# The gate product of a decoder's embedding step: tokens as one 512-column matmul, the sample's tokens as narrow matmuls

## The chip, the cores and the metric

The kernel runs on one core of one Trainium2 chip. The metric is the device time of one execution in microseconds. A core has a matrix engine (TensorE, PE in the profile, with PEld for its weight loads), VectorE (DVE), ScalarE (ACT), GpSimd (POOL) and SyncE (SP), which here issues nearly all DMAs. Each engine has its own instruction stream, run in order; the streams wait for each other by semaphores.

## The reference

One step of a decoder with two layers. The same weights are applied to 512 prompt tokens and to 8 x 4 = 32 sample tokens. The mixing part (a state-space scan and windowed attention) stands between two half-step FFNs; behind them comes a per-layer input embedding, whose gate is what is changed here:

```python
def _layer(h, pe, ssm0, conv0, k_past, v_past, pos0, lp):
    h = h + (0.5 * _swiglu(_rmsnorm(h, lp['g_ffn1']), lp['w1_a'], lp['w3_a'], lp['w2_a'])).astype(hd)
    ...
    h = h + mix.astype(hd)
    h = h + (0.5 * _swiglu(_rmsnorm(h, lp['g_ffn2']), lp['w1_b'], lp['w3_b'], lp['w2_b'])).astype(hd)
    gate = jax.nn.sigmoid(_rmsnorm(h, lp['g_ple']) @ lp['w_ple_gate'])
    h = h + (gate * (pe.astype(hd) @ lp['w_ple_proj'])).astype(hd)
    return h, ssm_new, conv_new, k_new, v_new
```

`w_ple_gate` is 1024 x 1024 and `w_ple_proj` 256 x 1024 in each layer. All data is float32.

## The kernel before

Features lie on the 128 partitions, tokens along the free dimension: the residual stream `h` is a tile of 128 x 8 x 544, eight slices of 128 features, and 544 = 512 prompt tokens followed by 32 of the sample. Every large product treats the 544 tokens together.

Precision comes from splitting. A float32 operand x is kept as a high part in float32r (XH) and the remainder in float32r (XL); a weight as `wh` and `wl`. A product is three matmuls per slice of 128 rows: wh with XH, wh with XL, wl with XH (`terms3`). The weights come by `piece`: a DMA into `raw`, a cast on ScalarE (`wh`, line 95), a difference on VectorE (`wl`, line 96); `raw`, `wh` and `wl` have three buffers each, so a piece waits for the release of the one three before it.

`gemm` (line 113) splits the 544 columns into two halves of 272, each in a PSUM bank of its own (a bank holds 512 float32 columns; eight banks rotate). A full product against the norm's output, `xgemm`, is 8 slices x 3 terms x 2 halves = 48 matmuls of 272 columns for one tile of 128 output features.

The norm's gain is folded in XH and XL (`Norm.split`, lines 140 and 142); the factor 1/rms is applied afterwards, by multiplying the product with `Rb`, a tile of 128 x 544 (`evac_r`, line 127: two multiplies of 272 columns). `Norm.sums` and `Norm.spread` make `Rb` with small matmuls while TensorE goes on.

The embedding stage, `ple`, runs over 8 tiles of output features. For each: the gate's `xgemm` (48 matmuls); the embedding's projection against EH and EL (12 matmuls of 272 columns); `evac_r` of the gate; a tanh on ScalarE (line 1061), since a sigmoid is made from a tanh; two multiplies with the projection (line 1063) and the addition to `h` (line 1064). In layer 1 the tile before is transposed back and stored (`store`, line 1041 and on). The stage runs once per layer, so there are 16 gate tiles. Behind layer 0's stage comes layer 1's first FFN, whose norm splits all eight slices of `h` again into XH and XL; slice 7 is the one that the last gate tile writes.

The program order is not kept word for word: a scheduler places each engine's instructions, so steps of neighbouring tiles interleave. The lists of instructions below show what it made.

Other parts hold matmuls of other widths that the trace can be asked about: line 414 (attention scores, 64 rows in two halves of the array, 128 or 256 columns), lines 671 and 805 (512 columns, scan and sample state), lines 801 and 156 (8 columns and 1 column).

## Time and profile before

| | |
|---|---|
| measured time, median of 2 runs | 2278.16 us (2277.71 to 2278.62) |
| span of the profiled execution | 2277.4 us |
| TensorE matmul busy | 2243.9 us, 99% |
| TensorE weight loads busy | 2191.8 us, 96% |
| VectorE busy | 1161.2 us, 51% |
| ScalarE busy | 699.0 us, 31% |
| GpSimd busy | 379.7 us, 17% |
| mean granted TensorE clock | 0.989 |

The profiled execution is told by its span alone, from its first to its last instruction; no time around it is given, and the measured median stands 0.76 us above it. A row of a group gives line, engine, operation, the tile written and the tiles read, the shape (partitions x elements, for a matmul rows*columns of the weights and then what moves) and a count. In a timeline row the first number is the start and the second the time until the last of the merged instructions ended. A matmul's single time includes its passage through the array: matmuls that follow each other overlap, so the pace is read from the distance of starts or of ends, not from the mean duration.

### The profile page before, as it was taken

The page shows a single profiled execution, that of the slowest core. Times are in us where ns is not written, and L with a number is a line of the kernel's source. Part 1 is how long each engine was busy: PE and PEld are TensorE (multiplying, and loading weights), DVE is VectorE, ACT ScalarE, POOL GpSimd, SP SyncE. Part 2 cuts the span into 40 slices and gives each one's busy share as a digit, 9 for nine tenths or more (in the row PEclk, how much of TensorE's full clock was granted, in tenths as well). Part 3 has the DMA queues.
Part 4 walks back from the last instruction along what each step waited for, and adds up shares of the span by engine and source line. Part 5 has one row for each costly group of instructions (what it writes and reads, how often), then busy time and mean ns, then how long its engine had stood idle before and what let it go on. Part 6 is the DMA issues. An engine that isn't in the chain of part 4 may idle for free.

```text
span 2277.4 us, 41580 instructions
## 1 busy us (share of the span) xinstructions
PE 2243.9 (99%) x17666; PEld 2191.8 (96%) x17666; DVE 1161.2 (51%) x2064; ACT 699.0 (31%) x1126; POOL 379.7 (17%) x361
## 2 busy tenths in 40 slices
PE   8999999999999999999999999999999999999999
PEld 8999999989899999999999999999898999999999
DVE  5443444389764433443554334434988544344434
ACT  4222223344342222223332222233443422222223
POOL 3000111233521100101110001113334211001110
PEclk9999999999899999999999999999999999999999
DMA  6323332422243323322233233233122432233223
GB/s 164 107 72 105 84 82 77 97 57 67 61 133 84 82 77 103 88 75 84 81 101 84 77 100 87 73 92 87 49 61 84 126 83 81 86 103 84 72 78 86
DMA packets 396357, 197.74 MB, mean 87 GB/s; under 512 B 35438, under 2 KB 395526, under 8 KB 396172
## 3 DMA queue, kind: packets, MB, share of 16 engines
q1 hardware_dynamic: 394588, 194.91, 31.2%
q8 instruction: 138, 2.26, 0.4%
q10 hardware_dynamic: 1584, 0.18, 0.1%
q14 instruction: 47, 0.39, 0.1%
HBM read 187.56 MB, written 9.53 MB: 87 GB/s over the span
## 4 chain that ended last, share of the span: by engine, by line
PE 92%; DVE 5%; ACT 1%; POOL 1%; DMA 1%; issue 1%; ACTq 0%; POOLq 0%; DVEq 0%
PE ps L113 86%; DVE CV L556 1%; DVE wl L96 1%; PE ps L801 1%; POOL acc L151 0%; DVE wk L419 0%; PE ps L691 0%; PE ps L324 0%; PE ps L450 0%; DVE CV L826 0%; PE ps L156 0%; DVE am L422 0%; PE ps L699 0%; PE ps L168 0%; PE ps L443 0%
## 5 line engine op out<-in xcount | busy, mean ns | idle before, releaser
L113 PE MATMUL ps<-XH,wh 128*128 128x272 f32 x3744 | 1087.3, 291 | 6.9 <-ACT wk L444 4.8
L113 PE MATMUL ps<-XL,wh 128*128 128x272 f32 x3744 | 1080.7, 289 | 3.0 <-DVE XL L142 3.0
L113 PE MATMUL ps<-XH,wl 128*128 128x272 f32 x3712 | 1073.5, 289 | 0.0
L95 ACT CAST wh<-raw 128x1024 fp32r<-128x1024 f32 (+4 forms) x400 | 361.6, 904 | 1293.2 <-issue 737.0
L113 PEld LDWEIGHTS ps<-XH,wh 128*128 128x128 f32 x3744 | 707.5, 189 | 12.0 <-ACT wk L444 5.2
L113 PEld LDWEIGHTS ps<-XL,wh 128*128 128x128 f32 x3744 | 708.7, 189 | 4.2 <-DVE XL L142 3.4
L113 PEld LDWEIGHTS ps<-XH,wl 128*128 128x128 f32 x3712 | 703.1, 189 | 0.0
L96 DVE TENSOR_TENSOR wl<-raw,wh 128x1024 fp32r<-128x1024 f32 (+4 forms) x400 | 426.0, 1065 | 349.9 <-ACT wh L95 346.4
L113 PE MATMUL ps<-UH,wh 128*128 128x272 f32 x1408 | 411.2, 292 | 0.0
L113 PE MATMUL ps<-UH,wl 128*128 128x272 f32 (+1 forms) x1408 | 411.2, 292 | 0.0
L113 PE MATMUL ps<-UL,wh 128*128 128x272 f32 x1344 | 386.3, 287 | 0.0
L235 POOL TENSOR_TENSOR th<-th,Rb 128x544 f32<-128x544 f32 (+1 forms) x88 | 120.6, 1371 | 1149.9 <-DVE th L234 1145.2
L113 PEld LDWEIGHTS ps<-UH,wl 128*128 128x128 f32 (+1 forms) x1408 | 265.2, 188 | 9.5
L113 PEld LDWEIGHTS ps<-UH,wh 128*128 128x128 f32 x1408 | 265.6, 189 | 8.2
L113 PEld LDWEIGHTS ps<-UL,wh 128*128 128x128 f32 x1344 | 253.7, 189 | 0.0
L271 DVE TENSOR_TENSOR u<-ps,th 128x272 f32<-128x272 f32 x168 | 73.8, 442 | 222.1 <-POOL th L235 127.6
L127 DVE TENSOR_TENSOR t<-ps,Rb 128x272 f32<-128x272 f32 (+1 forms) x176 | 77.0, 440 | 205.4 <-PE ps L113 189.4
L151 POOL TENSOR_TENSOR acc<-acc,sq 128x544 f32<-128x544 f32 x49 | 76.5, 1561 | 325.4 <-ACT sq L150 325.0
L296 DVE SCALAR_TENSOR_TENSOR h<-ps,h 128x272 f32<-128x272 f32 x128 | 56.5, 442 | 126.7 <-PE ps L113 123.6
L234 DVE SCALAR_TENSOR_TENSOR th<-th,t 128x544 f32<-128x544 f32 (+1 forms) x88 | 63.3, 719 | 7.0 <-ACT th L233 6.8
L233 ACT ACTIVATE th<-t 128x544 f32<-128x544 f32 (+1 forms) x88 | 57.5, 654 | 17.5 <-DVE t L127 17.3
L272 ACT CAST UH<-u 128x544 fp32r<-128x544 f32 x84 | 54.1, 644 | 25.8 <-DVE u L271 25.8
(339 smaller groups left out, 1700.3 us busy)
## 6 DMA issues: line engine op xcount, KB each, us to landing
raw<-in_w_a SPq DMA_DIRECT2D x84, 512.0 KB
raw<-in_w_b SPq DMA_DIRECT2D x84, 512.0 KB
raw<-in_w_in SPq DMA_DIRECT2D x30, 512.0 KB
raw<-in_w_a SPq DMA_DIRECT2D x32, 384.0 KB
raw<-in_w_b SPq DMA_DIRECT2D x32, 384.0 KB
raw<-in_w_ple_gate SPq DMA_DIRECT2D x16, 512.0 KB
raw<-in_w_a SPq DMA_DIRECT2D x16, 320.0 KB
raw<-in_w_a SPq DMA_DIRECT2D x20, 256.0 KB
```

What stands on the lines that cost most here:

```text
L95: A.copy(wh[:, 0:nk, :], raw[:, 0:nk, :])
L96: V.tensor_sub(wl[:, 0:nk, :], raw[:, 0:nk, :], wh[:, 0:nk, :].bitcast(F32))
L113: PE.matmul(ps[a][:, 0:HN], lhsT, rhs[:, a * HN:(a + 1) * HN], start=gi == 0 and i == 0, stop=gi == n - 1 and i == len(terms) - 1)
L127: V.tensor_tensor(dst[0:np_, HALF[a]], ps[a][0:np_, 0:HN], Rb[0:np_, HALF[a]], op=ALU.mult)
L151: add.tensor_tensor(self.acc, self.acc, sq, op=ALU.add)
L233: A.activation(th[0:np_, :], t1[0:np_, :], AF.Tanh, scale=0.5)
L234: V.scalar_tensor_tensor(th[0:np_, :], th[0:np_, :], 1.0, t1[0:np_, :], op0=ALU.add, op1=ALU.mult)
L235: G.tensor_tensor(th[0:np_, :], th[0:np_, :], Rb[0:np_, :], op=ALU.mult)
L271: V.tensor_tensor(u[:, HALF[a]], p3[a][:, 0:HN], s[:, HALF[a]], op=ALU.mult)
L272: A.copy(UH[:, j - j0, :], u)
L296: V.scalar_tensor_tensor(h[:, m, HALF[a]], ps[a][:, 0:HN], 0.25, h[:, m, HALF[a]], op0=ALU.mult, op1=ALU.add)
L556: V.scalar_tensor_tensor(cv, pc[:, w:w + 568], P["cw"][:, w * 8 + ch:w * 8 + ch + 1], cv, op0=ALU.mult, op1=ALU.add)
```

## The change

For the gate product alone, `xgemm` is replaced by a new function `wide`. The 512 prompt tokens go as one matmul of 512 columns into a bank `pw`: 8 slices x 3 terms = 24 matmuls. The 32 sample tokens are copied once per stage, high and low parts side by side, into a small tile `XS` (two VectorE copies). Against it each slice has two narrow matmuls into a bank `pn`: `wh` with both parts at once (64 columns), which leaves the high product in the first 32 columns and the low one in the next 32, and `wl` with the high part (32 columns), added to the first 32. The evacuation adds the two halves: ScalarE copies the low product into `sl`, VectorE adds the rest and multiplies by `Rb`; the prompt's 512 columns are multiplied by `Rb` in one instruction. All other products keep their two halves of 272. Comment lines that the change also drops are left out here.

```diff
+        XS = lp.tile([128, KD, 2, NS], F32R, tag="XS", name="XS", bufs=1)
+        V.tensor_copy(XS[:, :, 0, :], XH[:, :, NP:N].bitcast(F32))
+        V.tensor_copy(XS[:, :, 1, :], XL[:, :, NP:N].bitcast(F32))
+
+        def wide(p):
+            pw, pn = bank(), bank()
+            for k in range(KD):
+                for i, (lhsT, rhs) in enumerate(((p[0], XH), (p[0], XL), (p[1], XH))):
+                    PE.matmul(pw, lhsT[:, k, :], rhs[:, k, 0:NP], start=k == 0 and i == 0, stop=k == KD - 1 and i == 2)
+            for k in range(KD):
+                PE.matmul(pn[:, 0:2 * NS], p[0][:, k, :], XS[:, k].rearrange("p a n -> p (a n)"), start=k == 0, stop=False)
+                PE.matmul(pn[:, 0:NS], p[1][:, k, :], XS[:, k, 0, :], start=False, stop=k == KD - 1)
+            return pw, pn
+
         for m in range(KD):
-            pg = xgemm(first if m == 0 else piece(wg, 0, m * 128, KD))
+            pw, pn = wide(first if m == 0 else piece(wg, 0, m * 128, KD))
             if m == 0:
                 norm.sums()
             p = piece(wpj, 0, m * 128, 2)
...
             t1 = lp.tile([128, N], F32, tag="pt1", name="pt1")
-            evac_r(t1, pg)
+            sl = lp.tile([128, NS], F32, tag="sl", name="sl")
+            A.copy(sl, pn[:, NS:2 * NS])
+            V.tensor_tensor(t1[:, 0:NP], pw, Rb[:, 0:NP], op=ALU.mult)
+            V.tensor_tensor(sl, pn[:, 0:NS], sl, op=ALU.add)
+            V.tensor_tensor(t1[:, NP:N], sl, Rb[:, NP:N], op=ALU.mult)
             A.activation(t1, t1, AF.Tanh, scale=0.5)
```

In the changed kernel the wide matmuls are on line 1059, the narrow ones on 1061 and 1062, the evacuation on 1075 to 1078, the tanh on 1079.

First place: TensorE, the last tile of layer 1, where the gate's product ends. Before, the end of the second half and the first of the projection:

```order
L113 MATMUL ps<-XH,wh 128x272
L113 MATMUL ps<-XL,wh 128x272
L113 MATMUL ps<-XH,wl 128x272
L113 MATMUL ps<-EH,wh 128x272
L113 MATMUL ps<-EL,wh 128x272
```

Now:

```order
L1059 MATMUL ps<-XH,wh 128x512
L1059 MATMUL ps<-XL,wh 128x512
L1059 MATMUL ps<-XH,wl 128x512
L1061 MATMUL ps<-XS,wh 128x64
L1062 MATMUL ps<-XS,wl 128x32
```

The narrow matmuls of all eight slices stand in a block of 16 behind the 24 wide ones, so every slice's weights are loaded for them a second time; the projection follows.

Second place: ScalarE, the end of layer 0's stage, where the splits for layer 1's first FFN begin (`pt` is the gate's tile `t1`; the 1024-column casts are weights of that FFN). Before:

```order
L150 ACTIVATE sq<-h 128x544
L140 ACTIVATE XH<-h,pg 128x544 x4
L95 CAST wh<-raw 128x1024
L1061 ACTIVATE pt_12184<-pt_12184 128x544
L140 ACTIVATE XH<-h,pg 128x544 x3
L95 CAST wh<-raw 128x1024
L140 ACTIVATE XH<-h,pg 128x544
```

Now:

```order
L140 ACTIVATE XH<-h,pg 128x544 x7
L150 ACTIVATE sq<-h 128x544
L95 CAST wh<-raw 128x1024
L1075 COPY sl<-ps 128x32
L95 CAST wh<-raw 128x1024
L1079 ACTIVATE pt_12144<-pt_12144 128x544
L140 ACTIVATE XH<-h,pg 128x544
```

Seven of the eight splits now stand together, and the last tile's tanh stands behind both weight casts, not between them. On VectorE, too, the second weight difference moves ahead of that tile's multiplies with the projection:

```order
L1077 TENSOR_TENSOR sl<-ps,sl 128x32
L96 TENSOR_TENSOR wl<-raw,wh 128x1024
L1078 TENSOR_TENSOR pt_12144<-sl,Rb 128x32
L96 TENSOR_TENSOR wl<-raw,wh 128x1024
L1081 SCALAR_TENSOR_TENSOR pt_12144<-pt_12144,ps 128x272 x2
L1082 SCALAR_TENSOR_TENSOR h<-pt_12144,h 128x544
```

## The prediction

> **What bounds the kernel now.** The page comes first: its span, the busy time of TensorE, and the chain of waits by engine.

> ```profile
> span 2277.4 us, 41580 instructions
> PE 2243.9 (99%) x17666; PEld 2191.8 (96%) x17666; DVE 1161.2 (51%) x2064; ACT 699.0 (31%) x1126; POOL 379.7 (17%) x361
> PE 92%; DVE 5%; ACT 1%; POOL 1%; DMA 1%; issue 1%; ACTq 0%; POOLq 0%; DVEq 0%
> ```

> TensorE is busy 99% of the span and makes 92% of the chain. A change counts here if it moves the time that TensorE's own stream takes. The second view gives each engine's busy time in stretches: the embedding stage of layer 0, that of layer 1, and, for later, a stretch of layer 1's sample scan. The figure behind POOL is the granted clock.

> ```profile
> 1082.00:1145.10 63.10, 63.10 (x502) 62.71 (x502) 33.70 (x63) 25.94 (x40) 10.28 (x8) 1.00 0.31 88
> 2202.00:2271.00 69.00, 69.00 (x547) 68.10 (x547) 30.56 (x58) 21.13 (x38) 1.30 (x1) 1.00 0.29 82
> 1740.00:1748.00 8.00, 5.24 (x22) 4.94 (x23) 7.08 (x15) 3.15 (x6) 1.02 (x1) 0.64 0.13 40
> ```

> In both stages that the change touches, PE is busy for the whole stretch (63.10 of 63.10, 69.00 of 69.00) at clock 1.00; VectorE has half its time free, ScalarE more. So the unit of the sum is the pace of back-to-back matmuls. The chain, in order of time, gives it for layer 1:

> ```profile
> 2223.17 7.53 PE ps L113 x60
> 2230.70 0.44 PE ps L1041 x4
> 2231.14 0.11 PE ps L1043
> 2231.25 7.53 PE ps L113 x60
> ```

> One output tile is 60 matmuls of 272 columns, 48 for the gate and 12 for the embedding's projection: 7.53 / 60 = 0.1255 us each, so the gate product takes 48 x 0.1255 = 6.02 us. There are eight per layer, 16 in all, 96.4 us or 4.2% of the span.

> **The change, part by part: the wide matmuls.** 48 matmuls of 272 columns go; 24 of 512, 8 of 64 and 8 of 32 come. The columns are the same: 48 x 272 = 13056 = 24 x 512 + 8 x 96. What counts is the price of one matmul of each width. The trace has 512-column matmuls on operands of the same type (float32r) in pairs on lines 671 and 805. A timeline row of a pair runs from the first's start to the second's end; the row by line gives the shortest, median and longest single one.

> ```profile
> 563.26 0.73 PE L671 MATMUL ps<-R,selr 64*128 64x512 f32 x2
> L671 PE MATMUL ps<-R,selr x16: 383/442/502, 563.3 to 1719.8; 64*128 64x512 f32 x16
> 1755.47 0.71 PE L805 MATMUL ps<-Bm,XE 128*128 128x512 f32 x2
> L805 PE MATMUL ps<-Bm,XE x16: 390/475/774, 620.5 to 1768.1; 128*128 128x512 f32 x16
> 2222.93 0.37 PE L113 MATMUL ps<-XH,wh 128*128 128x272 f32 x1
> 2223.14 0.29 PE L113 MATMUL ps<-XL,wh 128*128 128x272 f32 x1
> ```

> The first of a run shows a longer time (its weights are not yet loaded), so I take the distance between the two ends. On L671: 0.73 - 0.502 = 0.228 us; on L805, with its median for the first: 0.71 - 0.475 = 0.235. The same method on the gate's own matmuls, the last two rows: (2223.14 + 0.29) - (2222.93 + 0.37) = 0.13, against the pace of 0.1255, so it holds. I take 0.228: the 502 ns of L671 belong to a first one for certain, while 475 is a median over first and second ones. 24 x 0.228 = 5.47 us. Bounds: adding the difference of the durations, (0.383 - 0.290) to 0.1255, gives 0.2185 and 5.24 us; scaling by columns, 0.1255 x 512/272 = 0.236, gives 5.67.

> [...]

> **The narrow matmuls.** Each still needs a load of 128 weight columns. Rows of lines 414 (two 64-row matmuls side by side, 128 columns moving, float32r) and 801 (8 columns moving, full array):

> ```profile
> 457.93 0.28 PE L414 MATMUL ps<-KK,QL 64*128 64x128 f32 x2
> 458.04 0.39 PE L414 MATMUL ps<-KK,QH 64*128 64x128 f32 x4
> 458.26 0.28 PE L414 MATMUL ps<-KK,QL 64*128 64x128 f32 x2
> 1753.93 1.69 PE ps L801 x16
> ```

> Pairs start 0.11 us apart (458.04 to 458.26 holds two), although 128 columns are under half of 272; and 8 columns still cost 1.69 / 16 = 0.106. At 128 columns and fewer the price no longer follows the columns: I read it as the slot of a weight load. I take 0.110: 16 x 0.110 = 1.76 us. Bounds: 0.1055, so 1.69; and the 272 pace as a full slot, 0.1255, so 2.01.

> So a tile's gate takes 5.47 + 1.76 = 7.23 us in place of 6.02: +1.21, and 16 tiles make **+19.4 us**. Bounds: 6.93 to 7.68, +14.6 to +26.6.

> **Evacuation.** Two multiplies of 272 columns go; one of 512, two of 32 and a ScalarE copy of 32 come. Nearest rows by form:

> ```profile
> L127 DVE TENSOR_TENSOR pt<-ps,Rb 128x272 f32<-128x272 f32 x32 | 13.9, 441 | 44.9 <-PE ps L113 44.9
> L806 DVE TENSOR_TENSOR wk<-wk,ps 128x512 f32<-128x512 f32 x16 | 10.3, 683 | 1.6 <-PE ps L805 1.6
> L548 DVE TENSOR_TENSOR tmp<-ps,Rb 128x32 f32<-128x32 f32 x16 | 2.9, 180 | 0.0
> L172 ACT COPY Rb<-ps 128x32 f32<-128x32 f32 x8 | 1.5, 191 | 0.0
> L1089 DVE COPY h<-ps 128x256 f32<-128x256 f32 x1 | 0.4, 424 | 0.7 <-PE ps L1087 0.7
> ```

> VectorE: 0.683 + 2 x 0.180 = 1.04 for 0.88; the wide multiply is done while the narrow matmuls run. Behind the last narrow one stand 0.191 + 0.180 + 0.180 = 0.55 us before the tanh, where 0.44 stood. Both lie under the 12 projection matmuls (1.51 us). Uncovered it shows only at the end of the kernel: +0.1 us. The two copies into XS (about 0.42 each by L1089) sit behind the last split of the norm, 5.5 us ahead of their first reader. SyncE's and GpSimd's instructions keep their order; the number of PSUM banks asked for is the same. The stop of XH's readers comes earlier (the narrow matmuls read XS), which costs nothing.

> **The edge from layer 0 to layer 1.** Here the order moves: seven splits of XH come together, and the tanh of the last tile falls behind a second weight cast. The new FFN's first matmuls need slice 7 of XH and XL, which needs that tile's h.

> ```profile
> 1136.94 14.31 PE ps L113 x113
> 1143.57 1.04 ACT L95 CAST wh<-raw 128x1024 fp32r<-128x1024 f32 x1
> 1144.51 0.66 ACT L1061 ACTIVATE pt<-pt 128x544 f32<-128x544 f32 x1
> 1144.91 1.23 DVE L96 TENSOR_TENSOR wl<-raw,wh 128x1024 fp32r<-128x1024 f32 x1
> 1146.04 0.79 DVE L1063 SCALAR_TENSOR_TENSOR pt<-pt,ps 128x272 f32<-128x272 f32 x2
> 1147.43 0.73 DVE L1064 SCALAR_TENSOR_TENSOR h<-pt,h 128x544 f32<-128x544 f32 x1
> 1148.07 2.18 DVE L142 SCALAR_TENSOR_TENSOR XL<-h,pg,XH 128x544 fp32r<-128x544 f32 x3
> 1148.19 0.75 ACT L140 ACTIVATE XH<-h,pg 128x544 fp32r<-128x544 f32 x1 [0.16 <-DVE h L1064]
> 1151.26 0.94 PE ps L156 x10
> ```

> Before, the last split ends at 1148.07 + 2.18 = 1150.25, some 6.8 after the gate's end, just in time: the 113 matmuls take 14.31 where 113 x 0.1255 = 14.18. After, counted from the gate's end: first cast 1.04 and small copy 0.19; two small VectorE steps with a weight difference between them, 0.18 + 1.23 + 0.18, to 2.8; the second weight difference 1.23, to 4.1; then 0.79 + 0.73 + 0.75 + 0.78 in a row, to 7.1. Needed at 1.51 + 42 x 0.1255 = 6.8. I add **+0.4 us**, once; bounds 0 and 1.

> The sum: 19.4 + 0.4 + 0.1 = 19.9 on the profiled span, 2277.4 to 2297.3. The measured median is 0.76 above the span, 2278.16: **2298 us**, +0.9%.

> **The rivals.** (1) *Wide matmuls overlap in a long run*, so that each holds TensorE no longer than a 272 one: 24 x 0.1255 + 1.76 = 4.77, -1.25 a tile, 16 of them -20: 2258. For it: no trace row has more than two wide ones in a row. Against: 272 columns show no such overlap over 60, and the pairs' ends stand 0.228 apart. 2%.

> (2) *The narrow ones are cheap*: their load costs what a load of 32 columns does. From the L156 row (8 full loads, 2 of 32 columns): (0.94 - 8 x 0.106) / 2 = 0.046, so 16 x 0.046 = 0.74 and 6.21 a tile, +3 in all: 2282. If widths alone were paid for, 6.02 again: 2278. Against: L414, same operand type. 4%. [...]

> (3) *Slower by over 2%: the granted clock drops.* In 1740 to 1748 it was 0.64, and a wide pair there took:

> ```profile
> 1746.19 1.20 PE L805 MATMUL ps<-Bm,XE 128*128 128x512 f32 x2
> ```

> Ends apart by 1.20 - 0.774 = 0.426 us. If the narrow matmuls left the array idle enough to lower the clock in every tile, 24 x 0.426 + 16 x 0.21 (the narrow price scaled alike) = 13.6, +7.6 a tile: 2400. It passes 2% (45.6 us) from four tiles of the 16 on: 19.9 + 4 x (7.6 - 1.2) = 45.5. Against: that stretch had PE busy 5.24 of 8.00; here PE never waits. 1%.

> That the instruction is split in two is excluded: L805 has one record for each of its 16.

> **How the numbers follow.** Forecast 93%, rivals 2, 4 and 1%. The forecast's bounds are 2278.2 + 14.6 = 2293 and 2278.2 + 26.6 + 1 = 2306. The lower end goes to 2291, since two runs of the same kernel differ by 0.9 us and rival 2 in part would end there; the upper to 2304, since 2306 needs the dearest price of both widths and the longest stall at once. The rivals outside hold 7%. Two per cent is about what a measurement of this kernel can tell from no change. The forecast and rivals 1 and 2 lie within it, rival 3 beyond. With one in a hundred on either side for what no case names: faster 0.01, same 0.97, slower 0.02.

> **What would show it.** Gate matmuls of 512 columns 0.22 to 0.236 apart; 16 narrow ones in 1.7 to 2.0 us; tiles of layer 1 repeating every 9.3 us in place of 8.08; the span longer by 15 to 27, nearly all of it between the embedding stages' ends; PE still busy 99%, clock 1.00 there. Wrong if narrow ones come at under 0.08, or wide ones at under 0.20, or if PE idles in these stages.

## The result and the profile after

The changed kernel took **2309.26 us** (2308.79 to 2309.73, two runs) against 2278.16: 1.0135 times the time before (95% interval 1.0116 to 1.0153). Measured again in more runs beside the kernel before, it took 2304.62 against 2277.61, 1.0126 times (1.0106 to 1.0146). It is slower, by 27 to 31 us, where 20 were forecast; 2309 lies above the range, which ended at 2304.

The page of the changed kernel, its span, engines and chain:

```profile
span 2307.9 us, 41362 instructions
PE 2273.7 (99%) x17538; PEld 2203.3 (95%) x17538; DVE 1165.9 (51%) x2084; ACT 699.3 (30%) x1142; POOL 379.8 (16%) x361
PE 91%; DVE 6%; ACT 1%; POOL 1%; issue 1%; DMA 1%; ACTq 0%; POOLq 0%; DVEq 0%
```

TensorE has 128 instructions fewer and is busy 29.8 us longer. The span is 30.5 us longer. Where that time lies shows when the chain of waits is read at the same places in both kernels. First the steady tile, layer 0, changed kernel (start, length, engine, line, count):

```profile
1104.44 5.61 PE ps L1059 x24
1110.05 0.03 PE ps L1061
1110.08 0.10 PE ps L1062
1110.18 0.12 PE ps L1061
...
1111.74 1.59 PE ps L113 x12
1113.34 5.61 PE ps L1059 x24
```

The 24 wide matmuls take 5.61, 0.2338 each. The 16 narrow ones take 1111.74 - 1110.05 = 1.69, and the projection behind them 1.59 where it took 12 x 0.1255 = 1.51. Counted together, the narrow ones cost 8.90 - 5.61 - 1.51 = 1.78, 0.111 each. (The first narrow matmul is charged only 0.03: the timeline has its weight load at 1109.66, where the last wide one starts, and the loads of the narrow ones behind it begin 0.11 apart, at 1109.89, 1110.00 and 1110.11. The first of the projection, behind a narrow one, is the one charged more: 0.21 from its start to the next, where 0.125 follows.) A tile repeats after 1113.34 - 1104.44 = 8.90 us, not 7.53: +1.37, and 16 tiles make 21.9.

Next the first tile of the stage, which has the norm's small sums (L156) behind the gate and the spread (L168) behind the projection. Before, then after:

```profile
1088.07 0.94 PE ps L156 x10
1089.00 1.70 PE ps L113 x12
1090.71 1.13 PE ps L168 x8
```

```profile
1089.82 1.03 PE ps L156 x10
1090.85 2.66 PE ps L113 x12
1093.51 1.50 PE ps L168 x8
```

The same twelve projection matmuls take 2.66 in place of 1.70. The stretches of 2 us around them, with the granted clock behind POOL, give the reason:

```profile
1088.00:1090.00 2.00, 2.00 (x20) 2.00 (x19) 0.00 (x0) 0.20 (x1) 0.00 (x0) 1.00 0.04 8
1090.00:1092.00 2.00, 2.00 (x16) 1.97 (x16) 0.65 (x4) 0.39 (x2) 0.82 (x1) 0.81 0.00 0
1092.00:1094.00 2.00, 2.00 (x11) 2.00 (x11) 0.00 (x0) 0.63 (x1) 0.57 (x2) 0.50 0.68 188
1094.00:1096.00 2.00, 2.00 (x11) 1.75 (x11) 1.56 (x2) 1.08 (x3) 0.00 (x0) 0.84 0.25 74
```

The granted clock falls to 0.50 for some 3 us, though PE counts as busy throughout (2.00 of 2.00 in each). It comes right behind 16 narrow matmuls and 10 sums, 1088.13 to 1090.85, 2.7 us in a row. In before the clock is 1.00 there (1088 to 1094), and in the changed kernel's steady tiles too (1100 to 1155). Layer 1 has the same (projection 2.97 us). Beyond the 1.37 of a steady tile this costs 1.3 us in each layer.

Third the edge to layer 1's first FFN. A timeline of PE there, with what ended its idle time, and the next full product, before (first fence) and after:

```profile
1152.19 6.22 PE ps L113 x48
```

```profile
1162.67 0.29 PE L113 MATMUL ps<-XL,wh 128*128 128x272 f32 x1
1163.24 0.39 PE L113 MATMUL ps<-XH,wh 128*128 128x272 f32 x1 [0.28 <-ACT XH L140]
...
1164.06 0.39 PE L113 MATMUL ps<-XL,wh 128*128 128x272 f32 x1 [0.17 <-DVE XL L142]
```

```profile
1165.90 7.74 PE ps L113 x48
```

Starts 0.57 and 0.46 apart (the second from a matmul at 1163.60) where 0.1255 is the pace: TensorE waits for slice 7 of XH and then of XL, with short gaps around, 1.0 us in all against the kernel before. What made slice 7 late stands on VectorE, the last tile's first small addition (L1077) behind three splits of XL (L142):

```profile
1155.20 3.27 DVE L142 SCALAR_TENSOR_TENSOR XL<-h,pg,XH 128x544 fp32r<-128x544 f32 x3
1158.40 0.18 DVE L1077 TENSOR_TENSOR sl<-ps,sl 128x32 f32<-128x32 f32 x1
```

Behind the wait the clock falls to 0.50 once more, and a product that took 6.22 takes 7.74. Both falls, at the first tile and here, last 3.41 us:

```profile
1091.24:1094.65 3.41, 3.41 (x18) 3.41 (x17) 0.50 (x3) 1.04 (x1) 1.33 (x2) 0.50 0.54 152
1166.33:1169.74 3.41, 3.41 (x18) 3.41 (x17) 0.95 (x1) 0.00 (x0) 2.09 (x2) 0.50 0.32 82
```

They begin 75.09 us apart, 22 times 3.413. The records of the granted clock show the same throughout the traces of before and of the changed kernel: the clock is 1.00 or 0.50, and every low spell wholly inside the run, 9 in before and 12 in the changed kernel, lasts 3.41, 6.83 or 13.65 us and begins on one grid of 3.41 us, that is, a whole number of such steps from the others. Where the grid lies relative to the kernel differs between two executions of the changed kernel: a step lies 1.6 us behind the start of the sums at this edge in one and 1.3 in the other.

Together: 21.9 + 2 x 1.3 + 1.0 + 1.5 + 0.1 at the end = 27.1. The remaining 3.4 of the trace's 30.5 lie in code that is the same in both kernels, mostly in layer 1's mixing. Between the same two small matmuls (the spread of the mixing's norm and the sums of the next norm), in before, in the changed kernel, and in a second execution of the changed kernel:

```profile
1556.84:1810.53 253.69, 244.35 (x1977) 229.14 (x1976) 199.31 (x446) 104.02 (x227) 92.06 (x101) 0.97 0.29 80
```

```profile
1572.06:1828.72 256.66, 247.36 (x1977) 232.25 (x1976) 199.30 (x446) 103.96 (x227) 91.97 (x101) 0.95 0.29 79
```

```profile
1570.87:1823.63 252.76, 243.07 (x1977) 228.01 (x1976) 199.39 (x446) 103.97 (x227) 91.97 (x101) 0.97 0.29 80
```

The first figure is the length: 253.7, 256.7 and 252.8, with VectorE's and ScalarE's work alike to 0.1 us and the granted clock 0.97, 0.95 and 0.97. What differs is TensorE's clock, in a stage that leaves the array idle now and then (PE is busy 244.35 of 253.69 us in before): these stretches hold 5, 7 and 4 spells of 3.41 us at clock 0.50. The second execution of the changed kernel, 2304.62 in all, has the same 27.1 us in the four places above; its span is 25.4 longer than before's, since 1.6 went the other way elsewhere, 0.9 of it in this stage.

### The profile page after: what moved, and what is told of

It reads as the page before. It is cut to its first block, busy times and chain, and to the rows that moved or that the text cites. A ratio compares the mean times of both kernels' runs of the same rounds, so it can differ in the third digit from the quotient of the medians.

```text
span 2307.9 us, 41362 instructions
## 1 busy us (share of the span) xinstructions
PE 2273.7 (99%) x17538; PEld 2203.3 (95%) x17538; DVE 1165.9 (51%) x2084; ACT 699.3 (30%) x1142; POOL 379.8 (16%) x361
## 4 chain that ended last, share of the span: by engine, by line
PE 91%; DVE 6%; ACT 1%; POOL 1%; issue 1%; DMA 1%; ACTq 0%; POOLq 0%; DVEq 0%
PE ps L113 80%; PE ps L1059 4%; DVE CV L556 1%; DVE wl L96 1%; PE ps L801 1%; PE ps L1061 1%; DVE wk L419 1%; DVE XL L142 1%; PE ps L1062 1%; PE ps L691 0%; POOL acc L151 0%; PE ps L324 0%; DVE am L422 0%; DVE CV L826 0%; PE ps L156 0%
## 5 line engine op out<-in xcount | busy, mean ns | idle before, releaser
L113 PE MATMUL ps<-XH,wh 128*128 128x272 f32 x3488 | 1014.1, 291 | 7.6 <-ACT wk L444 4.8
L113 PE MATMUL ps<-XL,wh 128*128 128x272 f32 x3488 | 1008.4, 290 | 3.1 <-DVE XL L142 3.1
L113 PE MATMUL ps<-XH,wl 128*128 128x272 f32 x3456 | 1001.0, 290 | 0.0
L95 ACT CAST wh<-raw 128x1024 fp32r<-128x1024 f32 (+4 forms) x400 | 361.3, 903 | 1309.0 <-issue 751.8
L113 PEld LDWEIGHTS ps<-XH,wh 128*128 128x128 f32 x3488 | 660.4, 189 | 12.9 <-ACT wk L444 5.2
L113 PEld LDWEIGHTS ps<-XL,wh 128*128 128x128 f32 x3488 | 661.3, 190 | 4.5 <-DVE XL L142 3.8
L113 PEld LDWEIGHTS ps<-XH,wl 128*128 128x128 f32 x3456 | 655.8, 190 | 0.2 <-DVE wl L96 0.2
L96 DVE TENSOR_TENSOR wl<-raw,wh 128x1024 fp32r<-128x1024 f32 (+4 forms) x400 | 425.9, 1065 | 370.2 <-ACT wh L95 367.7
L113 PE MATMUL ps<-UH,wh 128*128 128x272 f32 x1408 | 411.2, 292 | 0.0
L113 PE MATMUL ps<-UH,wl 128*128 128x272 f32 (+1 forms) x1408 | 411.2, 292 | 0.0
L113 PE MATMUL ps<-UL,wh 128*128 128x272 f32 x1344 | 386.3, 287 | 0.0
L113 PEld LDWEIGHTS ps<-UH,wl 128*128 128x128 f32 (+1 forms) x1408 | 265.2, 188 | 9.5
L113 PEld LDWEIGHTS ps<-UH,wh 128*128 128x128 f32 x1408 | 265.6, 189 | 8.2
L113 PEld LDWEIGHTS ps<-UL,wh 128*128 128x128 f32 x1344 | 253.7, 189 | 0.0
L127 DVE TENSOR_TENSOR t<-ps,Rb 128x272 f32<-128x272 f32 (+1 forms) x176 | 77.0, 440 | 204.0 <-PE ps L113 189.4
```

Source lines behind the costliest of these rows:

```text
L95: A.copy(wh[:, 0:nk, :], raw[:, 0:nk, :])
L96: V.tensor_sub(wl[:, 0:nk, :], raw[:, 0:nk, :], wh[:, 0:nk, :].bitcast(F32))
L113: PE.matmul(ps[a][:, 0:HN], lhsT, rhs[:, a * HN:(a + 1) * HN], start=gi == 0 and i == 0, stop=gi == n - 1 and i == len(terms) - 1)
L127: V.tensor_tensor(dst[0:np_, HALF[a]], ps[a][0:np_, 0:HN], Rb[0:np_, HALF[a]], op=ALU.mult)
```

## The experiments

Theory A: a matmul costs its columns (about 0.45 ns each) and only some 3 ns besides; a narrow one costs the slot of a weight load, 0.111 us; the rest is a granted clock of 0.50 for 3.41 us behind a stretch of narrow matmuls and sums, and a stall at the edge. The rivals stand in each expectation. Times of one table block, from one row "before" to the next, come from the same chip and share the runs of the kernel before. Where a median and a trace differ, mind that single runs of one kernel spread over 3 to 12 us.

| kernel | median us | ratio to before (95%) |
|---|---|---|
| before | 2278.0 | |
| wide_only | 2274.83 | 0.9982 (0.9972 to 0.9993) |
| halves256 | 2305.59 | 1.0123 (1.0108 to 1.0138) |
| narrow128 | 2305.74 | 1.0125 (1.0109 to 1.0140) |
| interleave | 2302.65 | 1.0111 (1.0096 to 1.0126) |
| before | 2277.61 | |
| changed kernel again | 2304.62 | 1.0126 (1.0106 to 1.0146) |
| sums_mid | 2301.40 | 1.0109 (1.0094 to 1.0124) |
| old_last | 2302.85 | 1.0108 (1.0095 to 1.0122) |
| shift121 | 2293.59 | 1.0069 (1.0056 to 1.0082) |
| before | 2277.5 | |
| before_narrow | 2284.54 | 1.0038 (1.0014 to 1.0062) |
| narrow8 | 2285.38 | 1.0037 (1.0023 to 1.0051) |
| mid_and_old | 2302.17 | 1.0107 (1.0089 to 1.0124) |

### The wide matmuls alone

```diff
-            for k in range(KD):
-                PE.matmul(pn[:, 0:2 * NS], p[0][:, k, :], XS[:, k].rearrange("p a n -> p (a n)"), start=k == 0, stop=False)
-                PE.matmul(pn[:, 0:NS], p[1][:, k, :], XS[:, k, 0, :], start=False, stop=k == KD - 1)
```

(`pn` then names a part of XS, so that the evacuation has something to read)

> Leaves out the 16 narrow matmuls of every gate tile (the sample's gate is then made from other data); the 24 wide ones and the whole evacuation stay. Theory A (the changed kernel's trace: a wide matmul holds TensorE for 0.234 us and a narrow one for a weight-load slot of 0.112): a tile's gate takes 5.61 us where the first kernel has 6.02, so 16 x (5.61 - 6.02) = -6.6, and the low-clock stretches behind the first tiles go too: about 2272. Theory B (the narrow ones are cheap, at most 0.05 us each, and the extra time lies in wide matmuls and waits): over 2290.

Measured 2274.83, 3.2 under before. The chain of its layer 0:

```profile
1096.52 5.60 PE ps L1059 x24
1102.11 1.52 PE ps L113 x12
1103.63 5.59 PE ps L1059 x24
```

A tile repeats after 7.11 us, 0.42 under the 7.53 of before, and no first tile has a low clock (1.00 from 1084.91 to 1146.28 in layer 0); the edge stall of 1.1 us stays. 16 x -0.42 + 1.1 = -5.6; the span of this trace is 5.3 shorter, the median 3.2, which is 3 above A's 2272 and within what the mixing stages vary by (2.3 more in layer 1's here). B, at over 2290, falls: the extra time of the change does lie in the narrow matmuls. It also bounds any version of this idea: the sample's product would have to cost less than 0.42 us a tile, under four weight-load slots, to break even. No such version was run.

### Halves of 256

```diff
-            for k in range(KD):
-                for i, (lhsT, rhs) in enumerate(((p[0], XH), (p[0], XL), (p[1], XH))):
-                    PE.matmul(pw, lhsT[:, k, :], rhs[:, k, 0:NP], start=k == 0 and i == 0, stop=k == KD - 1 and i == 2)
+            for a in range(2):
+                cs = slice(a * 256, (a + 1) * 256)
+                for k in range(KD):
+                    for i, (lhsT, rhs) in enumerate(((p[0], XH), (p[0], XL), (p[1], XH))):
+                        PE.matmul(pw[:, cs], lhsT[:, k, :], rhs[:, k, cs], start=k == 0 and i == 0, stop=k == KD - 1 and i == 2)
```

> As the changed kernel, but the 512 prompt columns go as two halves of 256 into the same bank: 48 matmuls in place of 24, narrow ones unchanged. Theory A (price of a wide matmul = about 2.8 ns + 0.451 ns per column, from 125.5 ns at 272 and 233.8 at 512): 24 more fixed parts of 2.8 ns a tile, 16 tiles, +1.1: 2310 to 2311. Theory B (the fixed part is 12 ns, as the prediction's 0.228 us implied): 24 x 0.0097 = 0.23 a tile and +3.7 to +4.6: 2313 to 2314. A granted-clock stretch that moves can add or take 1.5 us in either case.

```profile
1103.55 5.66 PE ps L1061 x48
1110.89 1.61 PE ps L113 x12
```

48 matmuls of 256 columns take 5.66, 24 of 512 take 5.61: the 24 further ones cost 0.05 us, 2 ns each. The whole time does not decide: 2305.59 lies below both figures, which were counted from 2309, and 1 us from the repeated 2304.62 is below what these medians tell. The tile settles it for A: the fixed part of a matmul is 2 to 3 ns, not 12. Merging two matmuls of 256 columns into one of 512 saves next to nothing here.

### Narrow matmuls of 128 columns, and half as many

```diff
-                PE.matmul(pn[:, 0:2 * NS], p[0][:, k, :], XS[:, k].rearrange("p a n -> p (a n)"), start=k == 0, stop=False)
-                PE.matmul(pn[:, 0:NS], p[1][:, k, :], XS[:, k, 0, :], start=False, stop=k == KD - 1)
+                PE.matmul(pn[:, 0:128], p[0][:, k, :], xk, start=k == 0, stop=False)
+                PE.matmul(pn[:, 0:128], p[1][:, k, :], xk, start=False, stop=k == KD - 1)
```

Here `xk` is XS[:, k] with four parts, high, low, high, low.

> As the changed kernel, but every narrow matmul moves 128 columns (the sample's parts twice) in place of 64 or 32. Theory A (a narrow matmul costs the slot of its weight load, whatever it moves up to about 240 columns): no change, 2309 plus or minus 2. Theory B (it costs by its columns): 16 tiles x 8 x (64 + 96) columns x 0.451 ns = +9.2: 2318.

```profile
1090.14 0.99 PE ps L156 x10
1091.13 1.70 PE ps L113 x12
...
1110.73 1.55 PE ps L113 x12
1112.28 5.60 PE ps L1061 x24
1117.87 0.06 PE ps L1064
...
1119.61 1.42 PE ps L113 x11
```

The narrow block takes 1119.61 - 1117.87 = 1.74 with over 2.5 times the columns; a tile repeats after 1119.61 - 1110.73 = 8.88. A holds, and B's 2318 falls (2305.74 is below A's 2309, as the changed kernel's own repeated median is). What was not expected is the first tile: its projection takes 1.70, as before the change. With more columns in the same slots the clock did not fall, in either layer.

`narrow8` leaves out the narrow matmul of the weights' low part:

```diff
-                PE.matmul(pn[:, 0:2 * NS], p[0][:, k, :], XS[:, k].rearrange("p a n -> p (a n)"), start=k == 0, stop=False)
-                PE.matmul(pn[:, 0:NS], p[1][:, k, :], XS[:, k, 0, :], start=False, stop=k == KD - 1)
+                PE.matmul(pn[:, 0:2 * NS], p[0][:, k, :], XS[:, k].rearrange("p a n -> p (a n)"), start=k == 0, stop=k == KD - 1)
```

> As the changed kernel, but only 8 narrow matmuls a tile (the weights' high part against both parts of the sample; the weights' low part against the sample's high part is left out). Theory A (0.112 us for every narrow one, on TensorE's path): 16 tiles x 8 x 0.112 = -14.3, and the block of 0.9 us ahead of the sums may no longer lower the clock, up to -2.6 more: 288 of each thousandth aside, 2288 to 2291 beside 2305 for the changed kernel. Theory B (they cost by columns): 16 x 8 x 32 x 0.451 ns = -1.8: 2303.

(The words "288 of each thousandth aside" are a slip and carry no number.)

```profile
1106.62 5.60 PE ps L1059 x24
1112.22 0.81 PE ps L1061 x8
1113.03 1.58 PE ps L113 x12
1114.61 1.61 PE ps L1059 x7
```

A tile repeats after 7.99 us in place of 8.90: eight narrow matmuls are worth 0.91, 0.114 each. Measured 2285.38, 19 below the changed kernel of the block above it in the table and 3 below A's figures; neither the first tiles (no projection over 1.71) nor the edge has a low clock in its trace (1.5 us that A did not count), and the rest is within what the mixing stages vary by. B, at 2303, falls.

### Interleaved

```diff
-            for k in range(KD):
                 PE.matmul(pn[:, 0:2 * NS], p[0][:, k, :], XS[:, k].rearrange("p a n -> p (a n)"), start=k == 0, stop=False)
                 PE.matmul(pn[:, 0:NS], p[1][:, k, :], XS[:, k, 0, :], start=False, stop=k == KD - 1)
```

(the two lines now stand in the loop of the wide matmuls)

> As the changed kernel, but each slice's two narrow matmuls stand behind that slice's three wide ones, not all 16 in a block (in the first tile of a stage only partly, since XS is ready late there). Theory A (one weight load can be hidden at a time, so a narrow matmul costs its slot wherever it stands): the tile keeps its 7.4 us, and only low-clock stretches can differ: 2305 to 2310. Theory B (the loads of scattered narrow ones are hidden behind wide ones, so they cost about 0.03 us): 16 tiles x 16 x 0.08 = -20: about 2289.

```profile
1109.01 0.79 PE ps L1059 x3
1109.80 0.03 PE ps L1060
1109.83 0.10 PE ps L1061
1109.93 0.79 PE ps L1059 x3
```

A slice takes 0.92 us: 3 x 0.234 = 0.70 for the wide ones and 0.22 for two narrow ones, part of it seen as a longer first wide matmul (0.79 for three). So the price follows the narrow matmul wherever it stands, and B falls. The first tiles show no low clock here either (no projection over 1.71), which fits 2302.65 beside 2304.62, though 2 us between medians of two blocks prove nothing by themselves.

### What lowers the clock

```diff
                     PE.matmul(pw, lhsT[:, k, :], rhs[:, k, 0:NP], start=k == 0 and i == 0, stop=k == KD - 1 and i == 2)
+                if mid and k == 5:
+                    mid()
```

(the loop passes the norm's sums as `mid` in the first tile, so that they no longer stand behind the narrow block)

> As the changed kernel, but the ten small matmuls of the norm's sums stand behind the 18th wide matmul of a stage's first tile, not behind the block of narrow ones. Theory A (narrow block plus sums, 2.8 us in a row with little work in the array, is what halves the granted clock for the next 3 us or so): no low-clock stretch in either first tile, 2 x 1.3 = -2.6 against the changed kernel of the same call; the sums themselves cost 0.1 to 0.2 more each. Theory B (the stretches have another cause, or a narrow block alone is enough): the projection of the first tile still takes over 2 us.

```profile
1082.38 0.94 PE ps L156 x10
1086.61 1.59 PE ps L113 x12
...
1159.97 6.22 PE ps L113 x48
```

The projection is back at 1.59 and the granted clock in 1080 to 1100 was 1.00, where the changed kernel had 0.91 in 1082 to 1100. Layer 1's projection takes 1.59 too, at 1.00 in 2215 to 2240: A. Measured 2301.40, 3.2 below the changed kernel of the same block, where A said 2.6; the intervals overlap, and part of what the trace gains lies at the edge, which this edit does not touch (6.22 in the last line, where the changed kernel had 7.74). The reverse, in the kernel before (`p_m` is the tile's weights):

```diff
             pg = xgemm(p_m)
             if m == 0:
+                px = bank()
+                for k in range(KD):
+                    PE.matmul(px[:, 0:64], p_m[0][:, k, :], XH[:, k, NP - 32:N], start=k == 0, stop=False)
+                    PE.matmul(px[:, 0:NS], p_m[1][:, k, :], XH[:, k, NP:N], start=False, stop=k == KD - 1)
                 norm.sums()
```

> The kernel before, unchanged but for 16 extra narrow matmuls (64 and 32 columns in turn, their result is not used) in the first gate tile of each stage, between the gate product and the norm's sums. Theory A (a block of narrow matmuls ahead of the sums is enough to halve the granted clock, with nothing else of the change): each block costs 16 x 0.112 = 1.79 itself and 1.3 through the clock, twice: +6.2, and the projection of the first tile takes over 2 us. Theory B (only the change as a whole does it): +3.6, projection 1.5 us.

```profile
1086.80 1.15 PE ps L156 x10
1087.95 3.02 PE ps L113 x12
```

The same twelve matmuls take 3.02 us, in both layers, with nothing of the change but a narrow block ahead of the sums. In the trace each block costs 3.0 us, 6.0 in all. The median is 7.0 higher with an interval of 3 to 14, which holds B's figure too; the trace decides for A.

All traces agree. In the five that have the 16 narrow matmuls directly ahead of the sums (the changed kernel twice, halves256, old_last, before_narrow) all ten first projections take 2.66 to 3.02; in the other eight none takes over 1.71. The place of the 3.41-us grid does not explain the difference: in the ten, the low clock begins 0.82 to 1.57 us behind the start of the sums, and by the grid of the other low spells in the same trace, a step lies there in both layers of narrow128 (1.32 and 1.42) and in layer 0 of interleave (1.18) as well, where the clock stays at 1.00. How long such a stretch has to be was not measured.

TensorE's record of busy time is full in the low spells (3.41 of 3.41 us in both fences above), and narrow128, which fills the same slots with 128 columns each, keeps its projection at 1.70. So what parts the two is how much the matmuls move, not gaps between them; this is argued from these runs and not tested further.

### The edge, and both repairs

```diff
-            pw, pn = wide(first if m == 0 else piece(wg, 0, m * 128, KD))
+            old = m == KD - 1
+            pw, pn = (xgemm if old else wide)(first if m == 0 else piece(wg, 0, m * 128, KD))
```

(with `evac_r` for the old tile)

> As the changed kernel, but the last gate tile of each stage has the old form (48 matmuls of 272 columns and the old evacuation). Theory A (the stall between layer 0's last tile and layer 1's first FFN comes from that tile's longer chain of small steps and casts, and the low clock behind it from the stall): 2 x 1.36 for the two tiles, 1.0 for the stall and about 1.5 for the clock: -5 against the changed kernel of the same call. Theory B (the stall comes from other things, such as the splits in one block): only the two tiles, -2.7.

```profile
1144.89 15.28 PE ps L113 x120
1160.17 0.94 PE ps L156 x10
1161.11 6.22 PE ps L113 x48
```

From the projection ahead of the last tile, through that tile, to the sums there are 120 matmuls in 15.28 us, 0.127 each: no stall, and the product behind it is at 6.22 again. In the trace the edge costs 0.0 where the changed kernel paid 1.0 and 1.5, and the two tiles 1.4 less each. The measured 2302.85 is 1.8 below the changed kernel, not 5: this trace has 3.0 more in layer 1's mixing than before. So the place is shown by the trace, and the median can't carry it.

Two things stay open. With the old tile the splits of XL stand behind its last steps again, so this run does not part A's chain of small steps from B's splits in one block; the lines at the edge above show the splits ahead of the small addition. And the low clock is not explained by the stall alone: halves256, interleave and sums_mid have the same stall (the four matmuls at its end take 0.77 and the sums 1.07 in each of them, as in the changed kernel), and their products take 6.24, 6.24 and 6.22. In the two traces of the changed kernel a step of the 3.41-us grid lies 1.6 and 1.3 us behind the start of those sums, in these three 0.9, 2.8 and 2.8. So the 1.5 us seem to hang on where the grid falls; no run tests that.

`mid_and_old` has both edits:

> The changed kernel with both repairs: the sums behind the 18th wide matmul of the first tile, and the old form for the last tile of each stage. Theory A (what is left then is the steady cost of the wide form alone): 14 tiles x 1.37 = +19.2, and 0.1 to 0.4 for the moved sums: 2297 to 2298, against 2305 for the changed kernel. Theory B (the parts overlap, and one repair takes the other's gain): 2300 or more.

Its two stages together cost 18.6 us more than before's in its trace, near A's 19.3 to 19.6. The measured 2302.17 looks like B, and is neither: its mixing stage of layer 1, untouched, took 7.2 us more.

```profile
1564.17:1825.06 260.89, 251.31 (x1977) 235.66 (x1976) 199.21 (x446) 104.01 (x227) 92.01 (x101) 0.94 0.28 78
```

### Chance in the mixing stage

```diff
+            if m == 4 and not last:
+                px = bank()
+                for i in range(121):
+                    PE.matmul(px[:, 0:HN], p_m[0][:, i % KD, :], XH[:, i % KD, 0:HN], start=i == 0, stop=i == 120)
             pg = xgemm(p_m)
```

> The kernel before, with 121 more matmuls of 272 columns ahead of the fifth tile of layer 0's embedding stage (their result is not used): a delay of about 15.2 us at that place, as the changed kernel has it when layer 1's mixing begins, and nothing else. Theory A (the low-clock stretch in layer 1's scan depends on when the scan falls, not on the change; and a matmul of 272 columns costs 0.1255): the time of before plus 15.2, with the scan of layer 1 longer or shorter by up to 3 us than in before, by chance. Theory B (the changed kernel's own operations lengthen the scan): plus 15.2, the scan as in before.

> The changed kernel again, in more rounds. In its trace 21.8 us lie in the 16 gate tiles, 5.3 at the edge and the first tiles of the stages (a stall of 1.0 and low-clock stretches), and 3.0 in the scan of layer 1, which is the same code in both kernels. Theory A (that last part is a low-clock stretch which falls here or there from one execution to the next): a median near 2306, single runs from 2303 to 2310. Theory B (it belongs to the change): 2309 again, with a spread under 1.5 us.

The shifted kernel's runs lie between 2288.5 and 2299.1, the changed kernel's between 2301.9 and 2314.2, all with the same instructions each time. Both expectations went A's way: the delay shows as 14.9 us in the stage, and layer 1's mixing, untouched, was 2.1 us longer than in before (255.82 at clock 0.96), while the changed kernel's own second execution had it 0.9 shorter. Layer 0's mixing, which runs ahead of anything that was edited, varies as well: 256.45 in before, 257.97 and 257.51 in the changed kernel, 254.52 in shift121.

What varies is the number of 3.41-us spells at clock 0.50 in the stage. Layer 1's mixing has 4 of them in the changed kernel's second execution (252.76 us), 5 in before (253.69), 6 in shift121 (255.82), 7 in the changed kernel's first (256.66) and 9 in mid_and_old (260.89): some 1.6 us each. Why an execution gets more or fewer was not settled. That the two runs that gave 2309 lie so near each other is within this spread. The repeated median, +27.0, is close to the 27.1 that the four places account for; that it agrees to 0.1 is luck, since the rest of a run moves by several us.

## Why the prediction was right or wrong

- **Sign and mechanism of the main term: right.** Narrow matmuls cost a weight-load slot: 0.110 forecast, 0.111 measured, in any place and at up to 128 columns.
- **The price of a wide matmul: mis-sized.** 0.228 was taken from the ends of a pair, 0.2338 measured, near the bound by columns (0.236). What was wrong was to read the pair on L671 (64 rows, first of a run) against the pair on L805 (0.235), and to ignore what the bound said: 0.1255 x 512/272 means a fixed part near zero, and halves256 shows 2 to 3 ns. 24 x 0.006 x 16 = 2.2 us, nearly all of the difference between +19.4 and 21.9.
- **Evacuation under the projection: right.** 0.1 us at the end, and elsewhere nothing but its part in the edge.
- **The edge: right in kind, too small.** 0.4 forecast, with a bound of 1; 1.0 measured. The steps from the small addition to XL's last split take 5.6 (1158.40 to 1164.00) where 5.9 were counted. What was wrong is their start: the prediction let VectorE begin once ScalarE's cast and copy were done, 1.2 behind the gate's end; it began 2.2 behind (1156.21 to 1158.40), because three splits of XL stood ahead in its stream.
- **The clock: the failed step.** The prediction put its price into a rival that needs *every* tile at a low clock, and gave it 1% with the ground that PE never waits in these stages; to the forecast itself it gave no term for the clock. PE was indeed busy all the time, and still the clock fell to 0.50, in the two places where narrow matmuls and the sums stand in a row, and behind the edge: 2 x 1.3 + 1.5 = 4.1 us. With the wide price and the edge as measured, the sum would be 19.9 + 2.5 + 0.6 = 23.0, or 2301, inside the range; the 4.1 take it to 2305, beyond 2304. The other 3 to 4 us of the first measurement are the low spells of the mixing, for which the range had no term either, and which spread the runs of the changed kernel over 12 us. So 2304 was too low an upper end.
- **Rivals 1 and 2: fell.** Wide matmuls do not overlap (0.2338 over 24), and the narrow ones are not cheap (0.111).

## What to carry to other kernels

In these runs a matmul with a full weight tile costs its columns at 256 to 512 of them (0.46 ns each) and the slot of its weight load at 32 to 128 (0.111 us). Splitting 544 columns as 272 + 272 keeps both halves, at 0.1255 us, above the load's slot; 512 + 32 puts a whole slot behind a few columns, and the saved instruction is worth 2 to 3 ns. And keep small matmuls apart: two short groups that were harmless alone, 1.7 us of narrow matmuls and 1.0 us of sums, halved the clock (1.00 to 0.50) for the full-size work behind them in ten of ten cases, while the busy row read 100%. And before you explain a few us, count the low spells: here each was worth some 1.6 us, and the same kernel had 4 of them in a stage one time and 7 the next.

## What the runs showed of the hardware that was not expected

The pace of full matmuls at granted clock 1.00 is 0.45 to 0.46 ns a column, at 256, 272 and 512 columns alike (5.66 / 48 / 256 = 0.461, 0.1255 / 272 = 0.461, 5.61 / 24 / 512 = 0.457).

In the changed kernel's first tiles a stretch of 2.7 us of narrow matmuls and sums stood ahead of 3.41 us at clock 0.50 (1091.24 to 1094.65), which cost 1.3 us; the same slots with 128 columns each, in narrow128, did not bring it on: the projection behind them took 1.70, as in before.
